# Second layer: twelve query and key slabs split during the value projection and kept in DRAM, keys of the first pair before its queries

## The chip, the cores and the metric

One core of one Trainium2 chip runs the whole program. The metric is the device time of one execution in microseconds (us). Before the change it is 2409.92 us, the median of three runs (2409.3 to 2410.89).

## What is computed

Two decoder layers over 1024 tokens of width 1024, in float32. The first layer mixes tokens by differential attention, the second by forgetting attention; after each comes a gated MLP with a short convolution. Only the second layer's mixer is touched:

```
q, k, v, f_logit = split(x @ w_in, [H * d, 2 * H * d, 3 * H * d])     # H = 16 heads, d = 64
log_f = log_sigmoid(f_logit + b_f)
c = cumsum(log_f, axis=1)                                             # per head, over the tokens
s = einsum('bhqd,bhkd->bhqk', qb, k) * scale + cb[..., :, None] - c[..., None, :]
p = masked_softmax(s, causal_mask(start, Q_BLOCK, S))
o = einsum('bhqk,bhkd->bqhd', p, v)
return o @ w_o
```

## The kernel before

**Products in three parts.** Every float32 operand is split into a high part in TensorE's faster 32-bit format and a low part, the rest. ACT writes the high part (line 93) and DVE subtracts it from the source for the low part (line 95). A product is then three matmuls (`mm3`): high by high (104), high by low (109), low by high (110).

**Slabs.** The weights of queries and keys lie in DRAM as slabs of 128 x 1024, one for each pair of heads and each kind: number 3p for the queries of pair p and 3p + 1 for its keys, p from 0 to 7. `ahead(i)` starts the load of slab i into one of two staging tiles (`wst`, line 117, on the queue of SyncE, called SP); `ready(i)` splits it into a tile `wh` and a tile `wl`, of which there are three each. Some probability tiles use wh and wl too (`ptile`).

**The second layer's mixer in stages.** `attention(1)` first runs `first_pair`. That calls `all_values`: the values of all heads are projected in 64 steps of six matmuls, for two halves of the heads (g) and four pairs of token tiles. Its table `at` says at which step other work is put in: the transpositions of the second half of x (into `xh`, `xl`), the splits of the second half's value weights (`cut(1, kt)`), the gate's logits (step 25, line 706) and their sums (step 48), and the splits of slabs 0 and 1 (steps 36 and 42). Each value tile is split and stored to DRAM (`vd`, line 474). The gate's weights `wf` lie in one of the three tiles called `pt` until the logits are done; the other users of pt come later: the attention splits its transposed probabilities into them.

After the values, `first_pair` projects queries and keys of the first pair: first token half of queries, of keys, then second half of queries, of keys. `result` evacuates each from PSUM, and `move_q` (291) and `move_k` (309) bring the parts to the partitions where the scores want them, by small DMAs on SP's queue. At the end come the loads of the pair's values (`load_v`, 483) and of its two decay rows (`load_c`, 750), which the scores read as two more rows of the key operand.

Then a loop over the eight pairs. The scores of a pair (591 and 592), the row minimum over masked scores on DVE (599), the exponential on ACT (767), the scaling on DVE (770, 771), the transposition on TensorE (1619), the split of the result into `pt` by ACT and DVE (93, 95) and the product with the values (1645, 1646) are worked off as a list of jobs; between jobs stand the 32 steps of the next pair's key and query projection (`project`), so that TensorE has work while a softmax is on its way. In `project` keys come first. With the first token half of a slab `ahead` is called for the slab that comes next, and with the second half `ready`.

**What sets the order.** The program gives each engine's instructions a place when it is built: an instruction whose tiles are free may stand ahead of the place of its line, earlier lines take a tile first. On the chip every engine works its own queue in that order, so whatever stands behind a waiting instruction waits too. GpSimd (POOL) has little to do in this stage; it copies the query tiles `qz` (583) for the scores.

Of the kernel before, what the change touches and what calls it, by code (L numbers as in the profile page):

```python
# [9 lines left out]
F32 = mybir.dt.float32  # L10
F32R = mybir.dt.float32r
# [8 lines left out]
P = 128  # L20
# [3 lines left out]
NP = 8  # L24
# [29 lines left out]
T_ST, N_R, N_A = 2, 4, 6  # L54
X0_A, X0_B, X1 = 2, 2.5, 13
W_V, FRAC = 1, 0
V_T, V_W, V_LD = 5, 8, 12
TT1 = 3


class Trunk:
# [276 lines left out]

    def ahead(self, i):

        if i < len(self.slabs):
            self.stage[i] = self.fetch(self.slabs[i])

    def ready(self, i):
        if i < len(self.slabs):
            self.w[i] = self.cut(self.stage.pop(i))

    def first_loads(self, pos):
# [68 lines left out]
    def first_pair(self, t):  # L417

        self.all_values()
        for c in range(2):  # L420
            for s in range(2):
                if c:
                    self.ready(4) if s else self.ahead(4)
                ps = self.mbank()
                self.dense(ps, *self.w[s], c)
                self.result(1, s, c, ps, None, t)
        self.load_v(0, t)
        self.load_c(0, t)

    def all_values(self):  # L430

        nc = self.nc
        self.vd = [self.dr.tile([P, KT, 4, 2, P], F32, name=f"vd{g}") for g in range(2)]
        own = lambda: self.qtile(0)
        high, low = [partial(self.wp.tile, [P, 1024], F32R, tag=t, name=t + "v") for t in ("wh", "wl")]
        other = partial(self.tmp, F32R, self.pp, "p")  # L440
        homes = ((own,) * 4 + (high, low) * 2, (other,) * 4 + (high,) + (own,) * 3)
        w, stage = {}, {}

        def cut(g, kt):
            if kt % 2 == 0:
                stage[g] = self.fetch(self.i["wv1"][g, kt // 2])
            hl = homes[g][kt]()
            w[g, kt] = hl[:, :512], hl[:, 512:]
            self.split(*w[g, kt], stage[g][:, kt % 2 * 512:kt % 2 * 512 + 512])

        at = [[] for _ in range(64)]
        for kt in range(KT):
            cut(0, kt)
            at[V_T + 2 * kt].append(partial(self.transposes, self.acc, 1, (kt,), True))
            at[V_W + 3 * kt].append(partial(cut, 1, kt))
        at[25] += [partial(self.gate_logits, 1), self.forget_gates]
        for s in range(2):
            at[36 + 6 * s].append(lambda s=s: self.w.update({s: self.weight(self.slabs[s])}))
        at[48].append(self.forget_sums)
        n = 0  # L460
        for g in range(2):
            for t0 in range(0, 8, 2):
                ps = [self.mbank() for _ in range(2)]
                for kt in range(KT):
                    for fn in at[n]:
                        fn()
                    n += 1
                    for j in range(2):
                        self.mm3(ps[j], *self.x_lhs(kt, t0 + j), *w[g, kt], kt == 0, kt == KT - 1)
                for j in range(2):  # L470
                    out = self.tmp(F32R)
                    parts = out.rearrange("p (a b d) -> p a b d", a=4, b=4)
                    self.split(parts[:, :, 0::3], parts[:, :, 1:3], ps[j].rearrange("p (a h d) -> p a h d", a=4, h=2))
                    nc.sync.dma_start(self.vd[g][:, t0 + j], out.bitcast(F32).rearrange("p (a h d) -> p a h d", a=4, h=2))

    def x_lhs(self, kt, tt):
        ts = slice(tt % 4 * P, tt % 4 * P + P)
        return self.xh[kt, tt // 4][:, ts], self.xl[kt, tt // 4][:, ts]
# [303 lines left out]
    def attention(self, l):  # L782

        nc = self.nc
        self.od = self.dr.tile([NP, P, 1024], F32, name=f"od{l}")
        tiles = lambda p: [self.qtile((p + l) % 2) for _ in range(7)] + (
            [self.lp.tile([P, 1024], F32R, tag="lg", name=self.nm("kl"))] if l else [])
        self.slabs = [self.i[f"w{l}"][s * NP + p] if s < 3 - l else None for p in range(NP) for s in range(3)]  # L790
        self.slabs += [self.i[f"wo{l}"][k] for k in range(8)]
        self.w, self.stage, self.queue = {}, {}, []
        self.ofs, self.fill = {}, None
        if l == 1:
            for h in range(2):
                for t in self.qz[h]:
                    nc.gpsimd.memset(t[64:66, :].bitcast(F32), 1.0)
            self.gate_logits(0)
        cur = tiles(0)
        self.first_pair(cur) if l else self.first_pair_rotary(cur)  # L800
        live, values = [], []
        for p in range(NP):
            nxt = tiles(p + 1) if p < NP - 1 else None
            if nxt is not None:
                self.fill, n = self.project(l, p + 1, nxt), 32 if l else 48
            else:
                self.fill, n = self.out_early(l), 64
            jobs = (self.diff_jobs if l == 0 else self.fox_jobs)(p, cur)
            done = 0
            if p == 0:  # L810
                for done in range(1, (EARLY if l else EARLY0) + 1):
                    self.step()
            total, acc, base = sum(j[0] + 1 + W_C for j in jobs) - (W_V * 12 if l == 0 else 0), 0, done

            def steps(goal):
                nonlocal done
                while done < min(goal - 0.5, n):
                    self.step()
                    done += 1

            for job in jobs:
                live, values = self.tick(live, values, job)
                w = job[0] + 1 + W_C - (W_V * self.coming(values) if l == 0 else 0)
                acc += w
                goal = base + (n - base) * acc / total
                steps(done + (goal - done) * FRAC)
                values = self.tock(values)
                steps(goal)
            while done < n:
                self.step()  # L830
                done += 1
            next(self.fill, None)
            cur = nxt
        self.fill, n = self.out_late(l), 12
        while live or values:
            live, values = self.tick(live, values, None)
            values = self.tock(values)
            for _ in range(min(n, T_ST)):
                self.step()
                n -= 1  # L840
        for _ in range(n):
            self.step()
        self.load_o(7, self.ofs[NP - 1])
        for _ in self.fill:
            self.pulse()
# [848 lines left out]
class Norm:  # L1694
# [19 lines left out]
    def tiles(self, t0, n=1):  # L1714
        k = self.k
        return (t0, [k.small(tag="nm") for _ in range(n)],
                *[k.small(n, f"n{j}", 4 if n == 1 else 1) for j in range(3)])
# [120 lines left out]
```

## Time and profile before

| | |
|---|---|
| median of the runs | 2409.92 us |
| the profiled execution | 2413.51 us |
| its span, first to last instruction | 2410.8 us |
| granted TensorE clock over it | 0.998 |
| data moved by DMA | 329.02 MB, 136 GB/s on average |
| value projection of the second layer | about 1185 to 1280 us of the span |
| first pair's queries and keys | about 1280 to 1302 us |
| attention of the pairs | from about 1302 us, 50 us a pair |

In the profile, PE is TensorE's matmuls and PEld its weight loads, which run beside them. A busy time is the time in which the engine shows an instruction; matmuls overlap, so a busy PE is not one at its peak. A row of the waits says which engine, tile and line waited, for whom, how long in all, how often and the longest. In the timeline a row has start, duration, engine, line, operation and tiles, and in brackets the idle time of that engine before it with what ended it. Window rows give the busy time and number of instructions of each engine, the granted clock, the busy share of the DMA engines and what they moved.

### The profile page before, as it was taken

The numbers are of one execution on the slowest core, as the hardware profiler recorded it, in microseconds if no ns is written. First come the engines' busy times: TensorE is split into PE (matmuls) and PEld (weight loads), VectorE is DVE, ScalarE is ACT, GpSimd is POOL, SyncE is SP. The second block draws the span as 40 slices with busy tenths as digits, with TensorE's granted clock in tenths as the row PEclk, the third lists the DMA queues.
The fourth block names the chain that finished last, engine by engine and source line by source line (L and its number), as shares of the span: only waits on it lengthen the run. The fifth ranks groups of instructions, "written<-read, shape, count | busy, mean of one in ns | idle before, by whom it ended". The sixth has DMA issues, their size and how long they took to land. (4 is left out here: it accounts for less than half of the span.)

```text
span 2410.8 us, 33786 instructions
## 1 busy us (share of the span) xinstructions
PE 2389.0 (99%) x11627; PEld 1981.5 (82%) x11627; DVE 1905.6 (79%) x3740; ACT 1259.6 (52%) x2381; POOL 199.8 (8%) x396
## 2 busy tenths in 40 slices
PE   9999999999999999999999999999999999999998
PEld 7888888778888888888888888888888888888886
DVE  5888888889987877777833888889899887777768
ACT  4656666556544445544523555666465444445434
POOL 2111111010000110100100100101010001110000
PEclk9999999999999999999999999999999999999999
DMA  6223333521433557866334333345223335559672
GB/s 185 67 78 96 88 86 108 188 90 61 171 118 120 128 135 209 250 224 212 131 136 136 86 82 88 91 113 178 90 81 139 123 118 131 132 144 314 197 227 104
DMA packets 159275, 329.02 MB, mean 136 GB/s; under 512 B 21328, under 2 KB 44880, under 8 KB 159104
## 3 DMA queue, kind: packets, MB, share of 16 engines
q1 hardware_dynamic: 147904, 305.83, 39.1%
q0 software_dynamic: 10912, 20.98, 5.4%
q8 instruction: 91, 1.49, 0.2%
q14 instruction: 80, 0.66, 0.1%
q10 hardware_dynamic: 288, 0.07, 0.0%
HBM read 202.60 MB, written 90.64 MB: 122 GB/s over the span
## 5 line engine op out<-in xcount | busy, mean ns | idle before, releaser
L104 PE MATMUL m<-xh,wh 128*128 128x512 f32 x640 | 260.2, 407 | 0.1
L104 PE MATMUL m<-xh,wo 128*128 128x512 f32 x656 | 255.7, 390 | 0.0
L109 PE MATMUL m<-xl,wo 128*128 128x512 f32 x656 | 255.6, 390 | 0.0
L110 PE MATMUL m<-xh,wo 128*128 128x512 f32 x656 | 255.2, 389 | 0.0
L110 PE MATMUL m<-xh,wl 128*128 128x512 f32 x640 | 252.3, 394 | 0.0
L109 PE MATMUL m<-xl,wh 128*128 128x512 f32 x640 | 251.0, 392 | 0.0
L599 DVE CUSTOM_DVE_ANT_0 s<-s,mask 128x384 f32<-128x384 f32 (+7 forms) x256 | 194.2, 760 | 26.6 <-PE s L592 25.8
L93 ACT ACTIVATE wo<-wg 128x512 fp32r<-128x512 f32 (+1 forms) x168 | 102.2, 609 | 168.6 <-PE m L110 141.7
L93 ACT ACTIVATE pt<-m 128x512 fp32r<-128x512 f32 (+3 forms) x285 | 131.5, 491 | 101.6 <-PE m L1619 96.1
L95 DVE TENSOR_TENSOR pt<-m,pt 128x512 fp32r<-128x512 f32 (+3 forms) x285 | 153.8, 557 | 26.3 <-ACT pt L93 24.5
L583 POOL CAST qz<-q 64x128 fp32r<-64x128 f32 x256 | 94.7, 373 | 820.0 <-PE s L592 710.8
L93 ACT ACTIVATE wo<-t 128x512 fp32r<-128x512 f32 x132 | 83.5, 632 | 126.8 <-PE m L110 81.0
L110 PEld LDWEIGHTS m<-xh,wo 128*128 128x128 f32 x656 | 123.1, 188 | 25.6
L104 PEld LDWEIGHTS m<-xh,wo 128*128 128x128 f32 x656 | 123.3, 188 | 24.9 <-ACT p L1312 0.2
L109 PEld LDWEIGHTS m<-xl,wo 128*128 128x128 f32 x656 | 123.3, 188 | 24.3
L110 PEld LDWEIGHTS m<-xh,wl 128*128 128x128 f32 x640 | 120.2, 188 | 26.0 <-DVE wl L95 0.8
L104 PEld LDWEIGHTS m<-xh,wh 128*128 128x128 f32 x640 | 120.5, 188 | 21.1 <-DVE pt L95 1.2
L591 PE MATMUL s<-q,q 128*128 128x512 f32 (+4 forms) x384 | 134.8, 353 | 1.8 <-ACT wst L637 1.6
L95 DVE TENSOR_TENSOR wo<-wg,wo 128x512 fp32r<-128x512 f32 (+1 forms) x168 | 110.5, 659 | 32.8 <-ACT wo L93 32.1
L109 PEld LDWEIGHTS m<-xl,wh 128*128 128x128 f32 x640 | 120.8, 189 | 18.9
L95 DVE TENSOR_TENSOR wo<-t,wo 128x512 fp32r<-128x512 f32 x132 | 90.7, 688 | 48.7 <-ACT wo L93 48.5
L104 PE MATMUL m<-q,wo 128*128 128x512 f32 x328 | 128.6, 392 | 0.0
(416 smaller groups left out, 6528.8 us busy)
## 6 DMA issues: line engine op xcount, KB each, us to landing
wb<-in_wd SPq DMA_DIRECT2D x142, 256.0 KB, 5.2
t<-in_wi SPq DMA_DIRECT2D x44, 512.0 KB, 4.5
ha<-ad SPq DMA_DIRECT2D x86, 256.0 KB, 5.3
wg<-in_wi SPq DMA_DIRECT2D x42, 512.0 KB, 4.0
ad<-t SPq DMA_DIRECT2D x40, 512.0 KB, 2.6
wst<-in_w SPq DMA_DIRECT2D x38, 512.0 KB, 3.6
ha<-sd SPq DMA_DIRECT2D x66, 256.0 KB, 3.9
q<-q SPq DMA_DIRECT2D x128, 128.0 KB, 2.3
```

What stands on the lines that cost most here:

```text
L93: self.high = nc.scalar.activation(hi, src, AF.Copy, scale=1.0 if scale is None else scale)
L95: self.low = nc.vector.tensor_tensor(lo, src, hi.bitcast(F32), op=ALU.subtract)
L104: last = mm(out, wh, xh, start=start, stop=False)
L109: mm(out, wh, xl, start=False, stop=False)
L110: mm(out, wl, xh, start=False, stop=stop)
L583: nc.gpsimd.tensor_copy(qz[r:r + 64, :], q[r:r + 64, qt * P:qt * P + P])
L591: nc.tensor.matmul(sb[:, ks], q[:, qt * P:qt * P + P], kd[:, ks], start=True, stop=False)
L599: self.nc.vector.tensor_tensor_reduce(sb[:, :ln], sb[:, :ln], self.mask[:, 1024 - ln:], 1.0, BIG, ALU.add, ALU.min, mn)
```

## The change

The slabs of queries and keys of pairs 3 to 8 (twelve slabs) are fetched while the values are projected, one every five steps from step 3 on, and split three steps later by the new `keep`. It splits into two pt tiles and stores both, 512 KB each, into DRAM tiles, on POOL's queue. Later `ahead` does nothing for such a slab, and `ready` loads the two parts straight into wh and wl, on SP's queue.

In `first_pair` the keys of both token halves now come before the queries; the decay rows and values are loaded between the two, the decay rows first. Slab 1 is fetched and split at step 36 and slab 0 at step 42, instead of the other way round.

```diff
-V_T, V_W, V_LD = 5, 8, 12
+V_T, V_W, V_LD, W_P = 5, 8, 12, 3
...
     def ahead(self, i):
 
-        if i < len(self.slabs):
+        if i < len(self.slabs) and i not in self.parts:
             self.stage[i] = self.fetch(self.slabs[i])
 
     def ready(self, i):
-        if i < len(self.slabs):
+        if i in self.parts:
+            self.w[i] = [self.wp.tile([P, 1024], F32R, tag=t, name=self.nm(t)) for t in ("wh", "wl")]
+            for t, part in zip(self.w[i], self.parts.pop(i)):
+                self.nc.sync.dma_start(t.bitcast(F32), part)
+        elif i < len(self.slabs):
             self.w[i] = self.cut(self.stage.pop(i))
...
         self.all_values()
-        for c in range(2):
-            for s in range(2):
-                if c:
-                    self.ready(4) if s else self.ahead(4)
+        for s in (1, 0):
+            for c in range(2):
+                if s == 0:
+                    self.ready(4) if c else self.ahead(4)
                 ps = self.mbank()
                 self.dense(ps, *self.w[s], c)
                 self.result(1, s, c, ps, None, t)
-        self.load_v(0, t)
-        self.load_c(0, t)
+            if s:
+                self.load_c(0, t)
+                self.load_v(0, t)
...
         for s in range(2):
-            at[36 + 6 * s].append(lambda s=s: self.w.update({s: self.weight(self.slabs[s])}))
+            at[42 - 6 * s].append(lambda s=s: self.w.update({s: self.weight(self.slabs[s])}))
         at[48].append(self.forget_sums)
+        for m in range(2 * NP - 4):
+            i = 3 * (2 + m // 2) + (1 - m % 2)
+            at[W_P + 5 * m].append(partial(self.ahead, i))
+            at[W_P + 5 * m + 3].append(partial(self.keep, i))
...
+    def keep(self, i):
+
+        hl = [self.tt.tile([P, 1024], F32R, tag="pt", name=self.nm("wk")) for _ in range(2)]
+        self.split(*hl, self.stage.pop(i))
+        self.parts[i] = [self.dr.tile([P, 1024], F32, name=self.nm("wk")) for _ in range(2)]
+        for part, t in zip(self.parts[i], hl):
+            self.nc.gpsimd.dma_start(part, t.bitcast(F32))
...
-        self.w, self.stage, self.queue = {}, {}, []
+        self.w, self.stage, self.parts, self.queue = {}, {}, {}, []
```

## Prediction

> **What bounds the kernel now.** I read the page's first part, then a table of windows over the second layer's start, then the waits of TensorE there, then the timeline at two places.
>
> ```profile
> PE 2389.0 (99%) x11627; PEld 1981.5 (82%) x11627; DVE 1905.6 (79%) x3740; ACT 1259.6 (52%) x2381; POOL 199.8 (8%) x396
> ...
> core 0: us, PE busy (x) PEld busy (x) DVE busy (x) ACT busy (x) POOL busy (x), PEclk, DMA share, GB/s
> 1190.00:1280.00 90.00, 90.00 (x414) 73.01 (x412) 30.98 (x56) 21.27 (x38) 1.63 (x2) 1.00 0.39 138
> 1280.00:1302.00 22.00, 22.00 (x99) 18.22 (x98) 4.53 (x6) 3.73 (x6) 1.05 (x4) 1.00 0.57 172
> 1302.00:1343.50 41.50, 40.58 (x209) 33.01 (x208) 31.00 (x81) 21.48 (x51) 4.91 (x16) 1.00 0.38 102
> 1443.50:1463.50 20.00, 19.66 (x109) 15.16 (x108) 16.41 (x46) 12.61 (x33) 2.31 (x8) 1.00 0.23 70
> 1463.50:1493.50 30.00, 30.00 (x159) 25.57 (x158) 24.29 (x54) 16.81 (x35) 2.47 (x8) 1.00 0.40 104
> ```
>
> The kernel is TensorE's from end to end, at a granted clock of 1.00 in every row. The values (first window row) and the first pair's keys and queries (second row) leave it no gap, while DVE has 59 us and ACT 69 us of their 90 free. In the attention that follows, a pair takes 50 us; the last two rows are one pair's first 20 and last 30 us. All of its 0.34 us of idle matmul time lies in the first 20, where DVE is busy 16.41 of 20 us. The waits of the weight loads show who is late:
>
> ```profile
> PEld m L1646 <- DVE pt L95: 9.3, 29, 0.4
> PEld m L1645 <- ACT pt L93: 6.5, 23, 0.4
> PEld m L1645 <- issue: 1.5, 4, 0.4
> ```
>
> These are the three largest waits from 1343.5 to 1643.5, six pairs: 17.3 us, 2.9 a pair, all for the split of transposed probabilities (pt). They overstate the loss, because a weight load may wait while the matmul before it still runs; the idle time above understates it, because a matmul counts 0.39 us though the next can start 0.23 us after it. So one place closely, with ACT's split of a slab in it and DVE's:
>
> ```profile
> 1443.84 0.45 PE L1645 MATMUL m<-pt,q 128*128 128x512 f32 x1
> ...
> 1444.39 0.50 PE L1646 MATMUL m<-pt,q 128*128 128x512 f32 x1
> 1444.39 0.19 PEld L1646 LDWEIGHTS m<-pt,q 128*128 128x128 f32 x1 [0.41 <-DVE pt L95]
> ...
> 1445.46 1.05 ACT L93 ACTIVATE wh<-wst 128x1024 fp32r<-128x1024 f32 x1
> 1446.12 0.40 PE L109 MATMUL m<-xl,wh 128*128 128x512 f32 x1
> 1446.35 0.39 PE L110 MATMUL m<-xh,wl 128*128 128x512 f32 x1
> 1446.41 0.53 ACT L93 ACTIVATE pt<-m 128x256 fp32r<-128x256 f32 x2
> 1446.58 0.40 PE L104 MATMUL m<-xh,wh 128*128 128x512 f32 x1
> 1446.83 0.39 PE L1645 MATMUL m<-pt,q 128*128 128x256 f32 x1
> 1446.83 0.19 PEld L1645 LDWEIGHTS m<-pt,q 128*128 128x128 f32 x1 [0.28 <-ACT pt L93]
> 1447.05 0.40 PE L109 MATMUL m<-xl,wh 128*128 128x512 f32 x1
> 1447.51 1.21 DVE L95 TENSOR_TENSOR wl<-wst,wh 128x1024 fp32r<-128x1024 f32 x1
> 1448.63 0.42 PE L592 MATMUL s<-q,qz 66*128 66x384 f32 x1
> 1449.50 0.54 DVE L599 CUSTOM_DVE_ANT_0 s<-s,mask 128x384 f32<-128x384 f32 x1
> ```
>
> L109 to L110 is the unhindered pace, 0.23 us. The first wait, 0.41, costs 0.55 - 0.23 = 0.32 us and stands ahead of the slab's split. The second, 0.28, stands right behind it: ACT was in the split until it took up pt. It costs little: the product starts 0.25 after L104 (0.02 late) and holds the next matmul 0.22 instead of about 0.11 for 256 columns. Together 0.13 us.
>
> **The change, part by part.**
>
> *Out of the attention.*
>
> ```profile
> L93 ACT ACTIVATE wh<-wst x12: 1047/1058/1083, 1318.7 to 1595.4; 128x1024 fp32r<-128x1024 f32 x12
> L95 DVE TENSOR_TENSOR wl<-wst,wh x12: 1204/1206/1219, 1324.0 to 1597.5; 128x1024 fp32r<-128x1024 f32 x12
> ```
>
> Twelve slabs are no longer split there: 12 x 1.06 = 12.7 us of ACT and 12 x 1.21 = 14.5 us of DVE go, none of it on TensorE's own path. Of a pair's two splits one falls where the window row has no idle TensorE (the last 30 us) and is worth nothing; the other falls in the first 20 us. There are six of that kind, in the pairs from 1343.5 to 1643.5. What one is worth: at least the 0.13 us behind ACT's part, at most the 1.21 us of DVE's part, if all that follows moves up. Between them is what DVE's part visibly holds up: the score that L592 finishes at 1449.05 is taken by L599 at 1449.50, 0.45 us later, and only some of that reaches a matmul. I take 0.3, nearer the low end, because the earlier wait of 0.41 us has no slab split ahead of it and is as long. 6 x 0.3 = 1.8 us.
>
> *Into the attention.* Each slab now comes as two loads of 512 KB, straight into wh and wl. They wait in SP's queue for the slab that held the slot; behind them stand the moves of the new keys and queries (L291, L309), wanted about a pair's length later except for the queries' first half. The traffic of a pair grows by 1 MB per 50 us, 21 GB/s on the 70 to 104 shown. I cost it at nothing: a slot comes free about half a pair, 25 us, before its slab is used. Without that cover a load stands in the open for about 4 us, as in the row of the staging loads further down.
>
> *Into the values.* Twelve times a load of 512 KB, ACT 1.06, DVE 1.21 and two stores of 512 KB from POOL's queue. ACT goes from 21.3 to 34.0 and DVE from 31.0 to 45.5 of 90 us: they fit. The data are 12 x 1.57 = 18.9 MB on top of 138 GB/s x 90 us = 12.4 MB, so 348 GB/s if all of it falls there. The busiest stretch of the first layer (945 to 1010, in 40 slices) shows that the DMAs can carry it:
>
> ```profile
> GB/s 369 299 252 260 300 367 354 291 405 400 405 393 391 386 280 296 323 258 335 139 303 256 313 291 362 405 403 410 378 400 386 381 271 173 190 314 9 29 158 108
> ```
>
> It reaches 400 and more for several slices. The Trainium skill (DMA: Bandwidth & Descriptors, Specifications) puts HBM's limit for one core at about 358 GB/s; by that the stretch would sit at the limit, with all transfers in it stretched. The slices differ from that figure, so they decide.
>
> What paces the twelve is the slots of pt. Both halves of a slab need one until their stores land; there are three, and the gate's weights (wf) hold one until the logits are done.
>
> ```profile
> L706 PE MATMUL m<-xh,wf x16: 387/397/402, 1181.5 to 1226.7; 128*48 128x512 f32 x16
> ...
> wst<-in_w SPq DMA_DIRECT2D x38, 512.0 KB, 3.6
> ad<-t POOLq DMA_DIRECT2D x4, 512.0 KB, 7.2
> q<-ql SPq DMA_DIRECT2D x32, 128.0 KB, 2.2
> ...
> 1192.90 1.14 SPq L117 DMA_DIRECT2D wst<-in_wv  x2
> ...
> 1302.18 0.60 ACT L93 ACTIVATE q<-m 128x512 fp32r<-128x512 f32 x1 [4.12 <-PE m L110]
> ```
>
> Staging slots are free at 1192.9, so the first split can start at 1192.9 + 3.6 = 1196.5. With a store from POOL at 7.2 us (the four of 512 KB), two slots give a slab per 1.06 + 1.21 + 7.2 = 9.5 us. Three slabs end at about 1225; then three slots give one per 9.5 x 2/3 = 6.3 us, and the eleventh split starts at 1196.5 + 28.5 + 7 x 6.3 = 1269. The key slab of the second pair (number 4) comes behind it in the staging slots: 2.3 + 3.6 + 2.3 more, 1277.5. TensorE wants it at 1302, when ACT takes the last half of the first pair's projections, so there are 24 us of cover. On the way ACT, in order, can wait for a store; behind it stand the splits of transposed x and the emptying of the value banks, whose tiles are wanted 6 and 11 us later. I cost this at nothing. The Trainium skill (DMA: Bandwidth & Descriptors, Anatomy of one DMA) fits a POOL-issued DMA by 2.0 us plus bytes over 436 GB/s, here an estimated 3.2 us; by that the twelve would be done some 30 us earlier. The row says 7.2, in heavy traffic, and is used.
>
> *Keys ahead of queries.*
>
> ```profile
> 1299.46 2.44 SPq L291 DMA_DIRECT2D q<-ql  x2
> ...
> 1307.42 0.22 PE L591 MATMUL s<-q,q 128*128 128x128 f32 x1
> 1307.97 0.40 SPq L750 DMA_DIRECT2D q<-cd  x1
> 1311.10 0.40 PE L592 MATMUL s<-q,qz 66*128 66x128 f32 x2
> 1311.36 0.30 DVE L599 CUSTOM_DVE_ANT_0 s<-s,mask 128x128 f32<-128x128 f32 x1 [2.42 <-PE s L592]
> ```
>
> The first score's second matmul (L592) stands 3.7 us behind its first (L591), for the decay rows (L750) that are issued last. The change issues them half the first pair earlier, about 11 us. TensorE filled that time with projection it needs anyway, so only what is missing as cover afterwards is won. The window from 1302 has 0.92 us of idle TensorE in 41.5, against 0.34 for a whole pair: 0.6 us more. In return the queries' first half is finished later, at the place that the second half of the queries has now. Its last move is issued by 1301.9 (the row at 1299.46) and lands 2.2 later, 1304.1, still 3.3 us ahead of L591. Bounds: a gain of 3.7 us, if the whole hold counts, and a loss of about 2 if the moves come late; I take a gain of 0.6, the row's excess.
>
> Sum: 1.8 + 0.6 = 2.4 us less. The profiled execution took 2413.51 us, its span 2410.8 with 2.7 around it; it becomes 2411.1. It lies 3.6 above the median of 2409.92, so the median becomes 2407.5. About 0.2%, 4.8 us, is what can be told from no change.
>
> **Rivals.**
>
> *DVE is the bound of a pair's first 20 us* (faster). For it: 82% busy, and half of the waits name DVE. Against it: it is not full, and most waits follow a transposition directly. Then each of six pairs gives back the whole 1.21 us: 7.3 + 0.6 = 7.9 us, 2402.0.
>
> *Stores too slow, the second pair's key slab late* (slower). If a store takes s instead of 7.2, the eleventh split starts at 1196.5 + (3 + 14/3) x (2.3 + s), and slab 4 is ready 8.2 us later. That passes 1302 from s = 10.4 us on. Two stores of 512 KB are always out together, besides loads, in a stretch at 348 GB/s. At 11.5 us TensorE stands about 8.7 us; less the 2.4 won, 6.3 slower: 2416.2. Against it: 7.2 was measured in the traffic of the slices above.
>
> *The change takes away work that was hidden anyway.* The waits are the plain latency from transposition over split to product; no gain, no loss: 2409.9.
>
> **How the numbers follow.** Forecast 0.42, DVE-bound 0.26, late slab 0.20, nothing 0.12. The forecast's own range is 2405 to 2409.5 (0.13 to 0.7 us a split, the start at 0 to 1 us). The whole range, 2400 to 2417, takes in the DVE-bound case and the late slab at its price; longer stores and a full gain at both places are left out. Faster by over 0.2%: the DVE-bound case and a few of the forecast's best, 0.32. Within: the rest of the forecast and the case of nothing, 0.48. Slower: 0.20.
>
> **What would show it.** Right: no slab splits between 1318 and 1598, DVE in a pair's first 20 us at about 15.2 instead of 16.4, pairs of some 49.7 us, no waits from 1190 to 1302, L592 right behind L591 at the start. The DVE-bound case: pairs of 48.8. The late slab: TensorE waiting for wh or wl at about 1302, and store landings over 10 us. I am wrong if pairs get longer, which none of the steps foresees, or if ACT's queue in the values makes TensorE wait on xh, xl or the value banks.

## The result, and the profile after

The changed kernel takes 2425.05 us (median of 6 runs, 2423.24 to 2426.87). The kernel before took 2410.8 us in runs beside it (median of 6, 2409.3 to 2412.86). The ratio is 1.0058, with a 95% interval of 1.0045 to 1.0071, so the change costs about 14 us. The forecast was 2.4 us less, and its range ended at 2417: it was wrong, in sign too. The profiled execution took 2425.79 us, with a span of 2423.7 us at a granted clock of 0.996.

First comes the question of where the time went. The values end with their last store to vd, and the attention's length can be read from its loads of vd, two per pair. One row for each of these, first of before, then of after (duration min/median/max in ns, then the first and the last start in us):

```profile
L474 SPq DMA_DIRECT2D vd<-t x16: 319/320/340, 1201.3 to 1281.8; - x16
L483 SPq DMA_DIRECT2D q<-vd x16: 565/590/1370, 1293.7 to 1617.0; - x16
```

```profile
L483 SPq DMA_DIRECT2D vd<-t x16: 320/327/1012, 1201.7 to 1303.2; - x16
L500 SPq DMA_DIRECT2D q<-vd x16: 564/588/1127, 1309.7 to 1631.8; - x16
```

Both start storing values at the same time (1201.3 and 1201.7). The changed kernel stores the last at 1303.2 instead of 1281.8, so the values lose 21.4 us. Its last pair loads values only 14.8 us late (1631.8 against 1617.0), so 6.6 us are won back by then. So there are two effects of opposite sign: 21 us lost in the values, and some 6.6 us won in the attention. The span is 12.9 us longer; the other 1.9 us lie behind the last of these loads, where both programs have the same work to do. The windows of after, by the bounds that the prediction used for the values, the first pair's projections and the start, then one pair's first 20 and its last 28.8 us:

```profile
1190.00:1280.00 90.00, 75.23 (x325) 58.75 (x324) 42.04 (x66) 30.16 (x45) 14.86 (x26) 0.92 0.83 308
1280.00:1302.00 22.00, 22.00 (x93) 18.03 (x93) 2.79 (x5) 3.02 (x5) 0.00 (x0) 0.95 0.46 172
1302.00:1343.50 41.50, 41.45 (x199) 34.34 (x198) 17.21 (x48) 12.53 (x31) 4.12 (x14) 1.00 0.62 178
1461.90:1481.90 20.00, 19.86 (x115) 16.21 (x113) 16.18 (x46) 12.93 (x35) 2.30 (x8) 1.00 0.31 97
1481.90:1510.70 28.80, 28.80 (x154) 24.64 (x153) 22.71 (x51) 14.76 (x31) 2.46 (x8) 1.00 0.45 126
```

TensorE was busy all 90 us of the first row before; now it is busy 75.23. DVE and ACT are at 42 and 30 of 90 us, far from full, as forecast, and yet they are late. TensorE's waits from 1185 to 1310 (total, times, longest in us) name what is late:

```profile
PE m L104 <- DVE t L95: 6.1, 2, 5.9
PE s L1083 <- DVE xl L95: 4.6, 1, 4.6
PE m L723 <- DVE t L95: 3.3, 1, 3.3
PE m L755 <- DVE t L95: 0.7, 1, 0.7
```

Each of them is a matmul or a transposition that wants a bank of PSUM which DVE has not yet emptied. What held DVE and ACT themselves, from 1190 to 1285 (three views: the waits of DVE, those of ACT, and those of SP's queue, of which one row matters here):

```profile
DVE wk L95 <- DMA wk<-wk: 23.3, 7, 6.7
```

```profile
ACT wk L93 <- DMA wst<-in_w: 28.5, 8, 4.6
ACT wk L93 <- DMA wk<-wk: 12.0, 3, 5.7
```

```profile
SPq L117 <- DVE wk L95: 29.6, 10, 5.2
```

Here wk is the early split's tile. Its two halves wait 35 us for tiles whose stores have not landed, and the first half waits 28.5 us for slabs still being loaded. The last row is a reason why a slab can be late: its load (L117) is issued only when the early split before it has emptied one of the two staging tiles, and SP stands 29.6 us for that. The timeline around the first gap shows how such a wait reaches TensorE (start, duration, instruction, in brackets the idle time before it and what ended it):

```profile
1209.33 0.40 PE L110 MATMUL m<-wlv,xl 128*128 128x512 f32 x1
1209.56 0.40 PE L104 MATMUL m<-wlv,xh 128*128 128x512 f32 x1
...
1211.97 1.06 ACT L93 ACTIVATE wk<-wst 128x1024 fp32r<-128x1024 f32 x1 [5.67 <-DMA wk<-wk]
1212.93 0.58 ACT L93 ACTIVATE xh<-s 128x512 fp32r<-128x512 f32 x1
...
1214.51 1.23 DVE L95 TENSOR_TENSOR wk<-wst,wk 128x1024 fp32r<-128x1024 f32 x1 [6.68 <-DMA wk<-wk]
...
1215.66 0.68 DVE L95 TENSOR_TENSOR xl<-s,xh 128x512 fp32r<-128x512 f32 x1
...
1216.40 0.90 PE L1083 MATMUL s<-ident,acc 128*128 128x128 f32 x3 [4.60 <-DVE xl L95]
...
1219.02 0.63 PE L109 MATMUL m<-q,xh 128*128 128x512 f32 x1
1219.44 0.63 PE L110 MATMUL m<-q,xl 128*128 128x512 f32 x1
```

ACT stands 5.67 us for the high part's tile, then DVE 6.68 us for the low part's. Behind them in the same queues, in order, stand the splits of the transposed x (xh, xl), which need nothing of the early slabs. TensorE stands 4.6 us. Afterwards its matmuls start 0.42 us apart instead of 0.23: the clock has halved. Windows of 10 us of the same kernel, the seventh number the granted clock:

```profile
1210.00:1220.00 10.00, 5.40 (x19) 4.14 (x18) 4.82 (x7) 4.15 (x7) 1.06 (x2) 0.71 0.76 269
...
1230.00:1240.00 10.00, 6.70 (x23) 3.18 (x22) 5.58 (x7) 3.82 (x7) 2.12 (x4) 0.83 0.85 308
...
1270.00:1280.00 10.00, 3.13 (x11) 1.96 (x10) 5.20 (x8) 3.43 (x7) 2.13 (x4) 0.78 0.99 374
1280.00:1290.00 10.00, 10.00 (x40) 8.10 (x40) 0.04 (x1) 0.00 (x0) 0.00 (x0) 0.88 0.67 248
```

The three gaps each have a dip of the clock behind them. The waits sum to 14.7 us, which leaves 6.7 of the 21.4 us. Behind the gaps the granted clock is 0.50 from 1216.4 to 1220.9, from 1234.7 to 1238.0 and from 1279.1 to 1282.4, in all 11.1 us at half speed, worth about 5.6 of the 6.7; the last 1.1 us are not accounted for. The Trainium skill (TensorE: Matmul & The Clock Gate, Part 1) says that TensorE falls to half its clock after an idle window of about 3.4 us; that the clock fell in the gaps of 4.6 and 5.9 us agrees with it, and the last section comes back to a shorter one.

The gain in the attention is as plain. The same load of vd in two successive pairs, before and after:

```profile
1365.58 1.37 SPq L483 DMA_DIRECT2D q<-vd  x1
...
1415.57 1.31 SPq L483 DMA_DIRECT2D q<-vd  x1
```

```profile
1386.37 0.60 SPq L500 DMA_DIRECT2D q<-vd  x1
...
1435.14 1.13 SPq L500 DMA_DIRECT2D q<-vd  x1
```

A pair takes 48.8 us instead of 50.0.

### The profile page after: what moved, and what is told of

Its sections match the earlier page's. It is cut to its first block, busy times and chain, and to the rows that moved or that the text cites. A ratio compares the mean times of both kernels' runs of the same rounds, so it can differ in the third digit from the quotient of the medians.

```text
span 2423.7 us, 33921 instructions
## 1 busy us (share of the span) xinstructions
PE 2388.5 (99%) x11627; PEld 1984.0 (82%) x11627; DVE 1908.1 (79%) x3740; ACT 1260.8 (52%) x2381; POOL 209.1 (9%) x420
## 4 chain that ended last, share of the span: by engine, by line
PE 44%; DVE 4%; issue 4%; ACT 1%; POOL 1%; DMA 0%; DVEq 0%; POOLq 0%; SPq 0%; ACTq 0%
PE m L104 9%; PE m L110 9%; PE m L109 9%; PE s L110 3%; PE s L104 3%; PE s L109 3%; PE m L1636 2%; PE m L1663 2%; PE m L1662 1%; PE s L608 1%; PE s L609 1%; DVE pt L95 1%; POOL wk L491 0%; DVE s L616 0%; DVE xl L95 0%
## 5 line engine op out<-in xcount | busy, mean ns | idle before, releaser
L104 PE MATMUL m<-xh,wh 128*128 128x512 f32 x640 | 261.4, 408 | 0.5 <-DVE pt L95 0.4
L104 PE MATMUL m<-xh,wo 128*128 128x512 f32 x656 | 255.7, 390 | 0.0
L104 PEld LDWEIGHTS m<-xh,wo 128*128 128x128 f32 x656 | 123.3, 188 | 24.8 <-ACT p L1329 0.2
L104 PEld LDWEIGHTS m<-xh,wh 128*128 128x128 f32 x640 | 120.6, 188 | 20.6 <-DVE pt L95 1.7
L608 PE MATMUL s<-q,q 128*128 128x512 f32 (+4 forms) x384 | 134.2, 351 | 2.1 <-ACT wst L654 1.8
L95 DVE TENSOR_TENSOR wo<-t,wo 128x512 fp32r<-128x512 f32 x132 | 90.6, 687 | 49.1 <-ACT wo L93 48.9
L104 PE MATMUL m<-q,wo 128*128 128x512 f32 x328 | 128.6, 392 | 0.0
```

The lines of the kernel that those rows point to most:

```text
L95: self.low = nc.vector.tensor_tensor(lo, src, hi.bitcast(F32), op=ALU.subtract)
L104: last = mm(out, wh, xh, start=start, stop=False)
L608: nc.tensor.matmul(sb[:, ks], q[:, qt * P:qt * P + P], kd[:, ks], start=True, stop=False)
```

## The experiments

**Theory A:** the splits in the values are not paid for in busy time. They wait, at the head of in-order queues, for stores and loads; what is queued behind them is late, and TensorE stands and then runs slowly. The attention's gain is real and separate. **Rivals:** the attention gained nothing and what came back is slack (B); the first pair's new order costs something (C); the traffic alone delays the values (F). All ratios are to the kernel before, run beside each.

### The two halves apart

*Early splits kept, their parts not used:* `ready` and `ahead` are those of before.

```diff
...
-        if i in self.parts:
...
-        elif i < len(self.slabs):
+        if i < len(self.slabs):
             self.w[i] = self.cut(self.stage.pop(i))
```

> The twelve slabs are still loaded, split and stored while values are projected, but nothing reads the parts: the attention loads and splits its slabs as it did before. Keys first stays. Theory A (the splits' waits on ACT and DVE cost the values some 19 to 21 us, and the attention gave 7.3 us of it back, 6 pairs by 1.2 us from 50.0 to 48.8): slower than the changed kernel by about 7 us, 2432 us (2429 to 2436), with pairs of 50.0 us. Rival B (the attention gained nothing from the missing splits; what came back is slack that a late start gives by itself): the same time as the changed kernel, 2425 us, with pairs of 48.8 us.

Measured: 1.008 (1.0065 to 1.0095), 2431.71 us. Pairs are 50.0 us again. B falls.

*Parts used, but only one slab split early, and its parts loaded twelve times:*

```diff
...
-        for m in range(2 * NP - 4):
...
-            at[W_P + 5 * m].append(partial(self.ahead, i))
-            at[W_P + 5 * m + 3].append(partial(self.keep, i))
+        at[W_P].append(partial(self.ahead, 7))
+        at[W_P + 3].append(partial(self.keep, 7))
...
```

> One slab alone is split and stored while values are projected, and the attention loads the parts of that one slab for all twelve (the other eleven slabs' own weights are left out, so what is projected from them is another matrix). Keys first stays. Theory A: the values lose nothing, the attention gains 6 x 1.2 us: 2410.8 - 7.3 = 2403.5 us (2401 to 2406), granted clock 1.00 through the values. Rival B: 2410 us, pairs of 50.0 us. A third reading, that the reads of two parts in place of one slab cost the attention something which the pairs' period hides: above 2406 us.

Measured: 0.9963 (0.995 to 0.9976), 2403.67 us, pairs of 48.8 us. By the times the attention's gain is 8 to 9 us (6 to 12 by the interval). The trace puts it lower: from the last store to vd to its last load there are 328.7 us (1279.8 to 1608.5) against 335.2 before, 6.5 us less, as in the changed kernel, and 335.0 in the run above. The rest of the 8 to 9 is not found in the stretch that the change shortens. The values' loss, from the run above, is about 20 us.

*The first pair's order alone:* the twelve `at` entries are removed and nothing else.

> Only the order of the first pair is changed: keys ahead of queries, slab 1 at step 36 and slab 0 at step 42; no slab is split early. Theory A with the first working's term: within 2 us of before, 2410 us (2408 to 2412). Rival C (part of the loss is the order's own: the first scores wait for the query rows' moves, which now come last): 2413 us or more, with TensorE waiting between 1290 and 1320 us.

Measured: 0.9999 (0.999 to 1.0008), and no wait of TensorE from 1185 to 1340. Nothing is lost by the order, and a gain is not to be seen at this resolution; C falls.

### What in the values costs

*Loads and splits without the stores:*

```diff
...
-        for part, t in zip(self.parts[i], hl):
-            self.nc.gpsimd.dma_start(part, t.bitcast(F32))
+        if i == 7:
...
+            for part, t in zip(parts, hl):
+                self.nc.gpsimd.dma_start(part, t.bitcast(F32))
...
```

> The twelve slabs are loaded and split while values are projected as in the changed kernel, but only the first slab's parts are stored, and the attention loads those for all twelve (the other slabs' own weights are left out). What is missing is 11 x 2 stores of 512 KB: their time in the DMA queues, and the wait of the next split for its tile. Theory A1 (the tiles held until the stores land are most of the loss): the values lose 0 to 6 us, 2403.5 to 2409 us. Rival A2 (the wait for the slabs' loads, 28.5 us of ACT's waits in the changed kernel, or the added work on ACT and DVE itself is the loss): 2415 us or more.

Measured: 0.999 (0.9981 to 1.0), 2410.22 us, 6.5 us above the attention's gain alone. So the stores make 15 of the 21 us, and the rest is there without them. TensorE's waits and ACT's longest group in this run:

```profile
PE m L726 <- DVE t L95: 2.8, 1, 2.8
PE s L1086 <- DVE xl L95: 1.0, 1, 1.0
```

```profile
ACT wk L93 <- DMA wst<-in_w: 32.1, 12, 4.9
```

Without stores a split still waits for its slab's load, each of the twelve by 2.7 us on average, and blocks what is behind it. Traffic is not the only reason, for it is down to 219 GB/s from 308: here too SP stands, 24.2 us in 11, for staging tiles that the early splits have yet to empty before it can issue the loads.

*Seven tiles instead of three,* so that no split waits for a store; the tiles are those of the first pair, which are asked for after the values (for this `all_values` is called ahead of `first_pair`).

```diff
...
-        hl = [self.tt.tile([P, 1024], F32R, tag="pt", name=self.nm("wk")) for _ in range(2)]
+        hl = [self.qtile(1) for _ in range(2)]
...
```

> All twelve slabs as in the changed kernel, with the same loads and stores at the same steps, but the parts go through the seven tiles that the first pair's queries, keys and values take later, in place of the three tiles for transposed probabilities (the first pair's tiles are asked for only after the values). Traffic is the same; what is gone is a split's wait for the store of the one before it. Theory A1 (the held tiles make the stores' part of the loss): the run without stores gave 2410 us, so 2410 us (2406 to 2413), no waits of ACT or DVE on the stores. Rival F (with 350 to 370 GB/s the loads of slabs and value weights come late whatever the tiles): 2420 us or more, with ACT's wait for the slab loads grown beyond 28.5 us.

Measured: 1.0037 (1.0025 to 1.0048), 2422.68 us. ACT's waits:

```profile
ACT q L93 <- DMA wst<-in_w: 41.9, 12, 8.3
```

The waits for stores are gone, as they must be, but only some 5 us of time came back, since the waits for loads grew from 28.5 to 41.9 us. The tiles alone are not the stores' part; A1 as I had put it falls.

*The traffic by itself.* A first try put DRAM-to-DRAM copies at the splits' steps:

```diff
...
+        for _ in range(3):
+            self.nc.gpsimd.dma_start(self.dr.tile([P, 1024], F32, name=self.nm("wk")), self.slabs[i])
```

> One slab is split and stored; for the other eleven, at the steps of their splits, POOL's queue gets three copies of 512 KB from DRAM to DRAM in place of the load and the two stores: the same bytes, but no split and no tile held. The attention loads the one slab's parts for all twelve (the other eleven slabs' weights are left out). Theory A (the wait stands in ACT's and DVE's order, behind tiles and slabs): 2404 to 2406 us, clock 1.00. Rival F (the traffic alone delays the values' own loads of weights enough to stop TensorE): 2410 us or more, with TensorE waiting on the splits of value weights.

Measured: 1.012 (1.0105 to 1.0135), 2441.8 us, and it says nothing of the values: the 33 copies wait for nothing, so POOL issued them between 2.3 and 100.8 us of the span, where TensorE was busy 71 of the first 100 us instead of 98. A second try made each triple read the one before it, so that the copies ran from 1202 to 1277:

```diff
...
+        old = getattr(self, "chain", self.parts[10] * 2)
+        self.chain = [self.dr.tile([P, 1024], F32, name=self.nm("wk")) for _ in range(3)]
+        for new, src in zip(self.chain, old):
+            self.nc.gpsimd.dma_start(new, src)
```

> The traffic by itself, in place of the run whose copies ran in the first 100 us: one slab is split and stored; then eleven triples of 512 KB copies from DRAM to DRAM on POOL's queue, each triple reading the one before it, so that one triple follows the other through the values and into the first pair, with no split and no tile held. The attention loads the one slab's parts for all twelve (the other slabs' weights are left out). Theory A: TensorE does not wait, 0.9965 to 0.998 of the kernel before. Rival F (traffic at that rate delays the values' own loads and the first pair's slabs): 1.000 or more, with TensorE waiting on value weights or on wh and wl.

Measured: 1.0001 (0.9992 to 1.0009), 2411.84 us, 8 to 9 us above the attention's gain alone. TensorE's waits, ACT's, and the values' window:

```profile
PE s L1093 <- DVE xl L95: 5.4, 1, 5.4
```

```profile
ACT whv L93 <- DMA wst<-in_wv: 11.3, 2, 8.9
```

```profile
1190.00:1280.00 90.00, 84.56 (x382) 68.20 (x381) 30.10 (x55) 19.90 (x35) 19.05 (x37) 0.96 0.92 335
```

At 335 GB/s a load of value weights, issued by 1206.2, came so late that its split on ACT stood 8.9 us, to 1214.4, and the split of x behind it was late: the same kind of block, by traffic alone. So F holds too, for copies that run three at a time. The loss has two parts, both through ACT's and DVE's order: tiles held by stores, and loads that aren't there. How much of the second part is traffic, and how much the late issue for want of a staging tile, these runs don't separate.

*The stores from SP instead of POOL,* the changed kernel otherwise:

```diff
-            self.nc.gpsimd.dma_start(part, t.bitcast(F32))
+            self.nc.sync.dma_start(part, t.bitcast(F32))
```

> The changed kernel with the 24 stores issued by SP in place of POOL. Theory A1: a tile is held from the split to the landing; if SP's stores land sooner than POOL's median of 6.3 us, splits wait less and the loss shrinks, 2418 us (2412 to 2423). Against that, SP is in order too: a store that waits for DVE's part holds the loads queued behind it, and the loss may grow. Rival F (traffic): the same 2425 us.

Measured: 1.0005 (0.9996 to 1.0014), 2415.27 us: about 13 us of the loss gone with the same bytes (306 GB/s over the 90 us, against 308). TensorE's waits:

```profile
PE m L104 <- ACT wh L93: 4.9, 1, 4.9
PE m L723 <- DVE t L95: 1.6, 1, 1.6
```

In the values 1.6 us are left. The 4.9 us stand at 1304 to 1309, and there TensorE wants wh: that is the rival of the late slab in its place, with about half of its 8.7 us, though not by its cause, since the splits hardly wait for tiles. The trace gives no landing times for SP's stores. What it gives is the splits' waits for them, 4.9 us in 3 against 35.3 us in 10 with POOL.

*Both remedies:* seven tiles and stores from SP.

> All twelve slabs through the seven free tiles, with stores from SP: both remedies at once. Theory H with held tiles as the rest of the loss: what is left are the waits for the slabs' loads, as in the run without stores: 0.999 of the kernel before (0.998 to 1.000), and the last key and query slabs are no longer late at 1302 us. Rival (the loads wait longer, as they did with seven tiles and POOL, 41.9 us against 28.5): 1.001 or more.

Measured: 1.0009 (1.0 to 1.0018). Free tiles add nothing to the stores from SP; TensorE waits 0.7 us in the values and 3.9 us for wh after them.

### Which split the attention pays for

*Six key slabs only,* and *six query slabs only,* one each 10 steps (i = 3 * (2 + m) + 1, or without the + 1):

```diff
...
-            at[W_P + 5 * m].append(partial(self.ahead, i))
-            at[W_P + 5 * m + 3].append(partial(self.keep, i))
+            at[W_P + 10 * m].append(partial(self.ahead, i))
+            at[W_P + 10 * m + 3].append(partial(self.keep, i))
```

> Only the six key slabs of pairs 3 to 8 are split early, one each 10 steps from step 3; the six query slabs are split in the attention as before. Theory A (the attention's gain of 8 us comes from the one split in each pair's first 20 us, which is that of a key slab; the values' loss comes from the splits queued behind stores and loads): pairs of 48.8 us, and with a slab each 14 us the stores have landed before the next split, so that the loads' wait alone is left, half of the 6.5 us that the run without stores lost against the run with the attention's part alone: 2403.7 + 3.3 = 2407 us (2403 to 2411). Rival D (both of a pair's splits count alike): pairs of 49.4 us, 2411 us.

> Only the six query slabs are split early, one each 10 steps from step 3; key slabs are split in the attention as before. Theory A: no gain in the attention, pairs of 50.0 us, and the values' loss of the six-slab kind: 2411.5 + 3.3 = 2415 us (2411 to 2419). Rival D: like the six key slabs, 2411 us, pairs of 49.4 us.

Measured: 1.0036 (1.0024 to 1.0049) with the keys, 1.0016 (1.0006 to 1.0027) with the queries. The loads of vd in two pairs, keys first, then queries:

```profile
1374.70 0.59 SPq L500 DMA_DIRECT2D q<-vd  x1
...
1424.64 0.59 SPq L500 DMA_DIRECT2D q<-vd  x1
```

```profile
1374.56 0.60 SPq L500 DMA_DIRECT2D q<-vd  x1
...
1423.44 0.60 SPq L500 DMA_DIRECT2D q<-vd  x1
```

I had the slabs the wrong way round. One of a pair's two splits counts and the other does not, as theory A says and rival D denies, but it is the query slab's: 48.9 us a pair without it, 49.9 without the key slab's. In both runs TensorE still waits about 6 us once at the gate logits (L723), more than the loads' share I had allowed. That the run with the queries, 2416.91 us, lies in its range of 2411 to 2419 is luck: it gained in the attention, where no gain was expected, and lost more in the values than was allowed.

*Six late slabs,* first keys, then queries: behind the transposed x and the gate logits.

```diff
-V_T, V_W, V_LD, W_P = 5, 8, 12, 3
+V_T, V_W, V_LD, W_P = 5, 8, 12, 27
...
+            at[W_P + 6 * m].append(partial(self.ahead, i))
+            at[W_P + 6 * m + 5].append(partial(self.keep, i))
```

> The six key slabs are split early, but only after the transposed x and the gate logits are through: fetched each 6 steps from step 27, split 5 steps after the fetch instead of 3. Behind a waiting split then stand only the emptied value banks, wanted later. Theory A: no wait of TensorE before 1302 us, granted clock 1.00, the full gain in the attention: 2403.5 us (2401.5 to 2406). Rival E (the traffic, or a waiting split, holds up the value banks or the first pair's slabs in the same way wherever it stands): 2408 us or more.

> As the run with six late key slabs, with the six query slabs in their place: fetched each 6 steps from step 27 and split 5 steps later, through the three tiles of the changed kernel. The late key slabs lost about 3 us in the values (TensorE waited 2.4 us at the forget sums) and gained nothing; the early query slabs had pairs of 48.9 us. Both together: 2414.6 - 7 = 2407.5 us (2405 to 2410). If the pairs' gain depended on which slabs come early and not on the split in their first 20 us, it could differ; 2412 us or more would speak against the query slab's split as the one that counts.

Measured: 1.001 (1.0001 to 1.0019) with the keys, which lack the attention's gain; 0.9983 (0.9974 to 0.9993) with the queries, 2410.21 us where before ran at 2413.69 in that set. The queries come out as expected, some 6 us less than the keys: 2407.5 us beside the 2413.05 of the set before is 0.9977, inside the interval, although 2410.21 us itself lies just over the range. One wait is left in each, at the forget sums, 2.4 and 2.0 us, which is rival E's sign.

### Versions that gain

*Six query slabs loaded ten steps ahead into tiles of their own:*

```diff
...
+    def early(self, i):
+        self.stage[i] = self.qtile(1)
+        self.nc.sync.dma_start(self.stage[i].bitcast(F32), self.slabs[i])
...
```

> Only the six query slabs are split early, since those alone shortened the pairs. Each is loaded straight into one of the same seven tiles ten steps ahead of its split (one each 8 steps, loads from step 4, splits from step 14), and the low part is written over the loaded slab. So a split waits neither for its load nor for a store, and the two staging tiles are left to the value weights. Theory A: nothing of the values is held up, the pairs take 48.8 us: 2403.5 us (2401.5 to 2406), granted clock 1.00 up to 1302 us. Rival G (the added work of ACT and DVE by itself comes between a transposition and its split): 2407 us or more, with waits of TensorE on xl or on the values' parts while no early split waits.

Measured: 0.9996 (0.9986 to 1.0005), 2412.37 us. The pairs took 48.9 us. But with no staging tile to wait for, the six splits were placed far earlier than their steps: the stores were issued from 1139.8 to 1192.2, ahead of the values. TensorE lost its time there, busy 85.74 of the 90 us from 1100 to 1190 against 90.00 in the run with the order alone. The expectation failed on where the work went, so G isn't tested by it.

*The six query slabs with stores from SP,* late and then early:

> The six late query slabs with their stores from SP in place of POOL. With POOL they kept the pairs' gain (48.9 us) but lost 2.0 us of TensorE at the forget sums and some 2 us more to the clock behind it, in a stretch where twelve stores and six loads crowd into 40 us. Theory H (stores from SP land sooner, and in SP's order they hold back the next load, so that ACT and DVE seldom wait for a store): no wait of TensorE before 1302 us, 0.997 of the kernel before, that is 7 to 8 us faster (2403 where the kernel before takes 2411). Rival: the loads' wait alone still stops TensorE at the forget sums, 0.998 to 0.999.

> The six query slabs from step 3, one each 10 steps, with stores from SP. With POOL the same slabs made TensorE wait 6.2 us once, at the gate logits, and gave back 6 x 1.1 us. Theory H: the wait at the gate logits goes or falls below 2 us: 0.997 to 0.998 of the kernel before. Rival (the wait there was for the slab's load, which a store from SP leaves as it is): as with POOL, 1.001 to 1.002.

Measured: 0.998 (0.9972 to 0.9989), 2406.21 us late, and 0.998 (0.9971 to 0.9989), 2406.49 us early, where before took 2411.33. In neither does TensorE wait from 1190 to 1302; it is busy all 90 us of the values' window. The pairs take 48.9 us. These beat both kernels. For the late ones theory H's sign is there, no wait, but the time is the rival's 0.998: about 5 us are gained, not 7 to 8. The trace shows 6.0 us of it between the last store to vd and the last load (1280.8 to 1610.0). And since the work of six early splits stands in the values here and TensorE doesn't wait, rival G falls for six slabs.

*No early split at all:* the kernel before, with the query slab split at the first step of its pair's projection instead of the ninth.

```diff
...
-                (self.ready if c else self.ahead)(i if s else i + 4 if p < NP - 1 else 24)
+                if s == 0:
+                    (self.ready if c else self.ahead)(i + 4 if p < NP - 1 else 24)
+                    if c and p < NP - 1:
+                        self.ahead(i + 3)
+                elif c == 0:
+                    self.ready(i)
```

> The kernel before (queries first again, nothing split early, nothing stored) with one thing moved: a pair's query slab is fetched behind the next pair's key slab and split at the first step of its projection instead of the ninth, so that its 1.06 us of ACT and 1.21 us of DVE fall in the last 30 us of the pair before, where DVE has room, and not in its own first 20 us. Theory A, as the six late query slabs with stores from SP have it (only the place of the query slab's split counts, and 1.1 to 1.2 us of each pair is its price): pairs of 48.8 to 48.9 us and nothing lost in the values, 6 to 7 x 1.15 = 7 to 8 us, 0.9967 to 0.9975 of the kernel before. Rival (the split costs DVE its 1.2 us wherever it stands in a pair, since DVE is the bound of the pair as a whole): pairs of 50.0 us, 0.999 to 1.001.

Measured: 0.9979 (0.997 to 0.9988), 2406.42 us, so 5 us where 7 to 8 were expected, though the pairs are as short as expected (48.8 us in the windows below). A pair's two splits in this kernel's timeline:

```profile
1473.38 1.22 DVE L95 TENSOR_TENSOR wl<-wst,wh 128x1024 fp32r<-128x1024 f32 x1
1476.26 1.21 DVE L95 TENSOR_TENSOR wl<-wst,wh 128x1024 fp32r<-128x1024 f32 x1
```

Before, the query slab's stood alone, 4 us into its pair (the row at 1447.51 in the prediction); now it stands beside the next key slab's, in the last 30 us of the pair before. Five pairs of before and of this kernel, from a load of vd to the same load five pairs on, first the products with pt (busy us, mean ns over all their shapes, idle us before them):

```profile
L1645 PE MATMUL m<-pt,q 128*128 128x512 f32 (+1 forms) x120 | 43.5, 364 | 0.4
L1646 PE MATMUL m<-pt,q 128*128 128x512 f32 (+1 forms) x120 | 42.8, 373 | 1.3
```

```profile
L1652 PE MATMUL m<-pt,q 128*128 128x512 f32 (+1 forms) x120 | 42.8, 356 | 0.0
...
L1653 PE MATMUL m<-pt,q 128*128 128x128 f32 (+2 forms) x121 | 41.1, 357 | 0.6
```

And the two stretches as windows:

```profile
1365.60:1615.50 249.90, 248.23 (x1321) 203.59 (x1321) 203.49 (x491) 147.09 (x330) 23.90 (x80) 1.00 0.34 93
```

```profile
1366.90:1611.10 244.20, 243.57 (x1322) 204.09 (x1321) 203.90 (x491) 147.15 (x330) 25.02 (x80) 1.00 0.35 95
```

For the one shape 128x512 the means are 424 and 421 ns before, 415 and 403 here. DVE does as much as before (203.90 against 203.49 us) and ACT too, and the five pairs take 244.2 us instead of 249.9. So it is the place and not the work. In these pairs all that the twelve early splits won is to be had without storing anything. Over the whole attention, from the last store to vd to its last load, it is 4.7 us (1282.1 to 1612.6) of the 6.6; the missing part lies mostly at the start, between the loads of vd at 1312.6 and 1369.2: 56.6 us against 55.1 in the changed kernel.

## Why the prediction was wrong

**The step that failed** is "I cost this at nothing", said of ACT waiting for a store with the splits of the transposed x and the value banks behind it. It was the right mechanism: the prediction named it as what would prove it wrong, and the traces show it at L1083, L104, L723 and L755. Its price was set by comparing one wait of ACT with the cover of 6 and 11 us. Three things were missing from that comparison. The second half of each split is DVE's, which waits again, for the other tile, and longer (6.68 us behind ACT's 5.67). The sum gave only the first split a wait for its load; yet a load is issued only when a staging tile is free, and traffic can delay it further: ACT waited 28.5 us in 8 for the slabs, and in the run without stores such waits alone stopped TensorE. And a gap costs more than its length: behind each the clock halved, about 5.6 us in all. With the 14.7 us of waits that is 20.3 of the 21.4 us that stand in place of 0.

**"They fit"** was true of busy time, 42 and 30 of 90 us, and irrelevant: a queue that stands is as late as one that is full.

**The slots' pace** was about right. Stores from POOL were put at 7.2 us each; by the view of the early splits' tiles in the changed kernel they land earlier in the median:

```profile
DMA to landing us min/median/max: 2.9/6.3/8.8
```

The eleventh split started at 1269.1, where 1269 was forecast, and the last at 1274.3. So close a match is partly luck: the stores were shorter than the sum had them, and the waits for loads, which it left out, made up for it. The rival of the late slab did not come by way of slower stores. In the changed kernel TensorE never waits for that slab; it appears where the values are no longer held up (stores from SP), at 1304.

**That the DMAs can carry it** was read from slices of 400 GB/s. Those showed a rate, not that a load arrives on time at that rate. The changed kernel's values moved 308 GB/s, and a load was late at 335 in the run with chained copies.

**In the attention** the term was mis-sized. Not 0.3 us a split but about 1.1 us came back, 6.6 us by the trace where 1.8 were forecast. That is near the 7.3 us that the rival *DVE is the bound of a pair's first 20 us* gave for the six pairs. Each run moved ACT's 1.06 us and DVE's 1.21 us together, so that it is DVE's part which counts is not shown. One sign of the forecast failed as well: DVE was busy 16.18 us of a pair's first 20, not 15.2. Two readings misled. I held the idle time of TensorE, 0.34 us a pair, for what there was to win. But of the 5.7 us that five pairs gave back in the last experiment, 4.7 were counted as busy before (248.23 against 243.57): the matmuls on pt were 8 to 16 ns longer each on average. I read this as waiting for operands that is counted as busy time; that the same shape takes longer is what the rows show. And I took an early wait of 0.41 us with no split ahead of it as a sign that the split was not to blame. What was right: of a pair's two splits only the one in the first 20 us counts, and the parts' own loads, put at nothing, cost nothing there: from 1310 to 1650 no wait of TensorE names them.

**Keys ahead of queries** was given 0.6 us. L609, the former L592, does now stand right behind L608, the former L591 (1328.90 and 1328.85). In the run with the order alone, the idle time of TensorE from 1302 to 1343.5 fell from 0.92 to 0.16 us, but the time is the same within 0.1% (0.9999): a gain of 0.6 us is less than these runs can tell.

## What to carry to other kernels

Work that is added to an engine with room to spare is priced by what it waits for, not by its duration: list what is queued behind it in order, and give each of its waits, on every engine it touches, the latency that the loaded DMAs will have, counted from the moment at which the transfer can be issued. When a pair of operations is late only in one part of a loop, first try to move it to a part with room, as the last experiment did in a few lines; splitting six slabs ahead and storing them won no more (0.998 against 0.9979) and moved 12.6 MB more (341.60 against 329.02 MB). And a stage whose TensorE is 99% busy may still give back 2%: compare a matmul's duration where it waits with where it doesn't.

## What the runs showed of the hardware

A short gap can be enough to halve the clock. In the run with six late query slabs TensorE waited 2.2 us (2.0 and 0.2), and then (windows around it, the clock in the seventh column):

```profile
1259.00:1262.00 3.00, 1.15 (x5) 0.96 (x6) 3.00 (x6) 1.48 (x4) 1.00 (x2) 0.96 1.03 384
1262.00:1265.00 3.00, 3.00 (x9) 2.32 (x8) 0.78 (x2) 0.31 (x1) 0.00 (x0) 0.50 0.90 266
1265.00:1268.00 3.00, 3.00 (x15) 2.41 (x14) 0.00 (x0) 0.00 (x0) 0.00 (x0) 0.97 1.03 419
```

It ran at half speed for about 3.4 us, 9 matmuls in 3 us instead of 15, so a wait of 2 us cost nearly 4. Here the measurement differs from the window of about 3.4 us that the Trainium skill (TensorE: Matmul & The Clock Gate, Part 1) gives, and it decides. The length of a gap alone doesn't decide: a wait of 1.6 us in the run with stores from SP left the clock at 1.00, and so did one of 2.4 us, up to 1231.9, in the run whose parts are not used.

Stores of 512 KB from POOL landed after 6.3 us in the median, beside loads at 308 GB/s, and the same bytes issued by SP made the early splits wait 4.9 us in place of 35.3. Why is not settled: SP issues its stores in order with the loads, so that a late store also holds the next load back, and that may matter as much as how fast a store lands.
